# Loading the query weight of an expert layer by blocks of 32 partitions

## The chip, the cores and the metric

The kernel runs on one core of one Trainium2 chip. The metric is the device time of one execution in microseconds (us). A core has five engines that run their own instruction streams and meet at semaphores: TensorE (PE, with its weight loads shown as PEld), VectorE (DVE), ScalarE (ACT), GpSimd (POOL) and SyncE (SP), which here only issues transfers. Sixteen DMA engines move the data of all queues.

## The reference

Two layers of an encoder on 256 tokens of width 2048, in float32. Each layer adds the output of a mixer of three groups of attention heads, and then the output of an expert layer (PEER):

```
def peer_ffn(x, w_q, sub_keys, u, vv):
    q = (x @ w_q).reshape(bsz, s_len, 8, 2, 64)          # w_q: 2048 x 1024
    s = einsum('bshcd,cnd->bshcn', q, sub_keys)          # scores against 2 x 128 sub-keys
    ...                                                  # top 16 of 16384 experts for each head
    a = einsum('td,tkd->tk', xt, u[it])                  # u: 16384 x 2048
    return einsum('tk,tkd->td', gelu(a) * gt, vv[it])
```

The change touches only how `w_q` (8 MB for each layer) reaches the chip's memory.

## The kernel before

**Split products.** Every float32 operand of a product is split in two parts, `hi` (ACT, L251) and `lo` (DVE, L256; in part of the expert scan POOL). Three products (`hi` by `hi`, and each `hi` by the other's `lo`) make one float32 product.

**The job list.** The projections, the scan over the expert rows `u` and the start of the product with `v` are written as a list of jobs, which `run` works through. A job loads one tile `raw` of 128 partitions by 2048 elements (1 MB) and has two sub-steps, k = 0 and 1, each with half of the tile. Around the product of sub-step i the order in each engine's stream is: `hi` of sub-step i+2, `lo` of sub-step i+1, then the load of job j+2, then the matmuls of sub-step i. There are two `raw` buffers (in the scan every third tile comes from a third one), three `hi` and two `lo`. A load therefore waits until the last `lo` of two jobs before has read its buffer, and that `lo` waits for PE to be through with the `lo` two sub-steps before.

**The query projection.** In `proj_q` eight jobs load the query weight with `load_rows(..., strips=True)`, two k-tiles of 128 rows in each. The order of the rows is that of the transposed input: k-tile c holds the rows `a*512 + c*32 + j` for a = 0 to 3 and j = 0 to 31, so that the partition is `32*a + j`. In the first seven of the sixteen sub-steps PE also transposes a part of the normalised input (L335), which ACT and DVE split (L168, L169). Ahead of the stage stands the last step of the mixer's output projection: DVE adds the result to the residual (L837), ACT sums its squares (L277), and from these comes the scale that the first transposes need.

**The scan.** The next jobs load the expert rows `u`, 128 for each job, with four DMAs, one for each block of 32 partitions, each 32 partitions by four runs of 2 KB (L1333). DVE transposes blocks (L1268), and 24 matmuls for each sub-step follow (L1302, L1304). In the program's order the transpose of the first `u` tile stands on DVE ahead of the `lo` of the last query sub-step.

Of the kernel before, what the change touches and what calls it, by code (L numbers as in the profile page):

```python
# [33 lines left out]
P = 128  # L34
# [4 lines left out]
KT = D // P  # L39
# [55 lines left out]
def hybrid_parallel_heads_peer_encoder_kernel(ctx, tc, x, ln1, w_in, a_sink, b_rel_bias, c_q_norm, c_kv_norm,  # L95
# [4 lines left out]
    V, S, G, TE, SP = nc.vector, nc.scalar, nc.gpsimd, nc.tensor, nc.sync  # L100
# [162 lines left out]
    def load_rows(w, segs, c0, strips=False):  # L263

        def f(raw):
            wv = w.rearrange("(a c j) n -> c a j n", a=4, c=KT, j=32) if strips else \
                w.rearrange("(c p) n -> c p n", p=P)
            for k in range(2):
                o = k * 1024
                for s, n in segs:  # L270
                    SP.dma_start(raw[:, o:o + n], wv[c0 + k][..., s:s + n])
                    o += n
        return f
# [1277 lines left out]
```

## Time and profile before

| | |
|---|---|
| median of 3 runs | 3404.0 us (3401.57 to 3412.46) |
| the profiled execution's own time | 3402.82 us |
| its span, first to last instruction | 3401.0 us |
| mean granted clock of TensorE | 0.967 |
| PE / PEld busy | 91% / 84% |
| DVE / ACT / POOL busy | 72% / 50% / 54% |
| queue of SP's transfers | 434.08 MB, 52.3% of sixteen engines' span |

Busy shares are means over stages with different limits. The profile's page also gives the span in 40 slices; one slice is 85 us, about the length of one query projection, and there are two of these in the span, one for each layer.

### The profile page before, as it was taken

Reading aid. Unit: us, or ns where it says so; the run is one execution under the profiler, and the core shown is the slowest. Engines: PE = TensorE matmul, PEld = TensorE weight load, DVE = VectorE, ACT = ScalarE, POOL = GpSimd, SP = SyncE. Lnnn points to the kernel's source line nnn. Section 1 sums busy time; section 2 is a strip of 40 time slices with the busy share of each in tenths; the row PEclk is TensorE's granted clock in tenths of the full one; section 3 lists DMA queues with packets and bytes.
Section 4 is the critical chain, followed back from the end, with each engine's and each line's share of the span. In section 5 each row is a group of like instructions: output and inputs, shape, how many; then the busy total and the mean of one; then the engine's idle time right before and its main releaser. Section 6 shows DMA issues by size and latency. Waiting matters only on the chain. (4 is left out here: it accounts for less than half of the span.)

```text
span 3401.0 us, 58125 instructions
## 1 busy us (share of the span) xinstructions
PE 3100.9 (91%) x21677; PEld 2863.9 (84%) x21677; DVE 2442.1 (72%) x3613; ACT 1705.5 (50%) x2827; POOL 1825.2 (54%) x1135
## 2 busy tenths in 40 slices
PE   8998788989999987999999988799999999878998
PEld 8997688989899985888889977798899999867886
DVE  6576448997879865777766665489877788666776
ACT  5553433347657534555545544343475665345554
POOL 3010035678888883665530100256788888736663
PEclk9999889999999998999999999899999999889999
DMA  5677378889999996888745774688999999968885
GB/s 188 201 215 212 122 162 184 174 183 186 184 180 199 182 226 197 339 313 302 287 136 175 225 207 140 152 184 182 179 189 181 184 195 179 226 163 326 307 308 181
DMA packets 437750, 702.12 MB, mean 206 GB/s; under 512 B 103672, under 2 KB 236488, under 8 KB 413192
## 3 DMA queue, kind: packets, MB, share of 16 engines
q1 hardware_dynamic: 256016, 434.08, 52.3%
q0 software_dynamic: 112304, 228.13, 23.1%
q10 hardware_dynamic: 69064, 35.36, 4.3%
q8 instruction: 190, 3.11, 0.4%
q14 instruction: 176, 1.44, 0.2%
HBM read 627.95 MB, written 69.47 MB: 205 GB/s over the span
## 5 line engine op out<-in xcount | busy, mean ns | idle before, releaser
L1302 PE MATMUL acc<-x2h,hi 128*128 128x256 f32 x4096 | 1008.5, 285 | 28.2 <-ACT hi L251 15.3
L1044 POOL DMA_INDIRECT Gd<-g,idx x512 | 940.8, 1837 | 168.1 <-issue 151.6
L1302 PE MATMUL acc<-x2l,hi 128*128 128x256 f32 x4096 | 994.2, 281 | 0.0
L251 ACT ACTIVATE hi<-uT 128x1024 fp32r<-128x1024 f32 x512 | 543.6, 1062 | 729.0 <-DVE uT L1268 679.7
L1268 DVE STREAM_TRANSPOSE uT<-raw 128x1024 f32<-128x1024 f32 x512 | 635.2, 1241 | 324.9 <-DMA raw<-in_peer_u_dram 243.2
L1302 PEld LDWEIGHTS acc<-x2h,hi 128*128 128x128 f32 x4096 | 780.1, 190 | 34.7 <-ACT hi L251 20.0
L1302 PEld LDWEIGHTS acc<-x2l,hi 128*128 128x128 f32 x4096 | 779.8, 190 | 0.0
L1304 PE MATMUL acc<-x2h,lo 128*128 128x256 f32 x4096 | 581.4, 284 | 114.2 <-DVE lo L256 92.1
L1304 PEld LDWEIGHTS acc<-x2h,lo 128*128 128x128 f32 x4096 | 522.0, 190 | 134.5 <-DVE lo L256 104.6
L256 POOL TENSOR_TENSOR lo<-uT,hi 128x1024 fp32r<-128x1024 f32 x116 | 303.0, 2614 | 462.4 <-PE acc L1304 164.8
L166 DVE TENSOR_TENSOR vl<-vr,vh 128x1024 fp32r<-128x1024 f32 x356 | 426.2, 1224 | 145.9 <-ACT vh L165 140.4
L256 DVE TENSOR_TENSOR lo<-uT,hi 128x1024 fp32r<-128x1024 f32 x396 | 470.5, 1188 | 19.8 <-PE acc L1304 19.5
L165 ACT ACTIVATE vh<-vr 128x1024 fp32r<-128x1024 f32 x356 | 367.0, 1054 | 147.4 <-PE y L156 133.2
L256 DVE TENSOR_TENSOR lo<-raw,hi 128x1024 fp32r<-128x1024 f32 (+1 forms) x240 | 292.6, 1224 | 188.7 <-ACT hi L251 94.8
L152 PE MATMUL y<-vh,dh 128*128 128x512 f32 x1032 | 407.9, 395 | 20.3 <-ACT vh L165 14.1
L156 PE MATMUL y<-vh,dl 128*128 128x512 f32 x1032 | 406.5, 394 | 0.0
L251 ACT ACTIVATE hi<-raw 128x1024 fp32r<-128x1024 f32 (+1 forms) x240 | 246.6, 1035 | 317.7 <-DMA raw<-in_peer_w_q_dram 87.7
L1354 POOL DMA_INDIRECT vr<-in_peer_v_dram,iv x160 | 220.0, 1375 | 168.8 <-ACT vh L165 78.3
L161 PE MATMUL y<-vl,dh 128*128 128x512 f32 x1032 | 295.7, 393 | 0.2
L152 PEld LDWEIGHTS y<-vh,dh 128*128 128x128 f32 x1032 | 196.8, 191 | 65.0 <-ACT vh L165 23.9
L161 PEld LDWEIGHTS y<-vl,dh 128*128 128x128 f32 x1032 | 195.8, 190 | 43.4 <-DVE vl L166 2.4
L156 PEld LDWEIGHTS y<-vh,dl 128*128 128x128 f32 x1032 | 196.8, 191 | 41.1
(400 smaller groups left out, 4316.9 us busy)
## 6 DMA issues: line engine op xcount, KB each, us to landing
raw<-in_peer_u_dram SPq DMA_DIRECT2D x1024, 256.0 KB
raw<-in_w_in_dram SPq DMA_DIRECT2D x64, 512.0 KB
Gd<-z SPq DMA_DIRECT2D x32, 1024.0 KB
raw<-in_w_o_dram SPq DMA_DIRECT2D x32, 1024.0 KB
Gd<-at ACTq DMA_DIRECT2D x124, 256.0 KB
raw<-in_w_in_dram SPq DMA_DIRECT2D x64, 256.0 KB
raw<-in_peer_w_q_dram SPq DMA_DIRECT2D x32, 512.0 KB
raw<-in_w_in_dram SPq DMA_DIRECT2D x32, 416.0 KB
```

Of the source, the lines that this page charges most:

```text
L152: TE.matmul(o, lh, rh, start=start, stop=False, skip_group_check=shared)
L156: TE.matmul(o, ll, rh, start=False, stop=False, skip_group_check=shared)
L161: TE.matmul(o, lh, rl, start=False, stop=stop, skip_group_check=shared)
L165: S.activation(hi, src, AF.Copy)
L166: V.tensor_tensor(lo, src, R32(hi), op=OP.subtract)
L251: S.activation(view(h), src, AF.Copy)
L256: (eng or V).tensor_tensor(view(lo), src, R32(view(h)), op=OP.subtract)
L1044: d = G.indirect_dma_start(out=Gd[:], out_offset=bass.IndirectOffsetOnAxis(ap=r["idx"][:, hf, i:i + 1], axis=0), in_=r["g"][:, hf, i:i + 1 ...
L1268: V.transpose(t.rearrange("p (c e i) -> p c e i", c=8, e=4), rv.rearrange("p e (c j) -> p c e j", c=8))
L1302: TE.matmul(o, hi[:, c * P:(c + 1) * P], xx, start=k == 0 and c == 0 and n == 0, stop=False)
L1304: TE.matmul(o, lo[:, c * P:(c + 1) * P], xT(k * 8 + c)[0], start=False, stop=k == 1 and c == 7)
L1354: G.indirect_dma_start(out=raw, out_offset=None, in_=peer_v.rearrange("l e d -> (l e) d"), in_offset=at_(r[iv][:, c, m:m + 1]))
```

## The change

The query weight's job is loaded with four DMAs instead of two. Before, each k-tile is one DMA whose source has the dimensions 4 (a), 32 (j), 1024 (n) and whose destination is all 128 partitions of one half of `raw` (512 KB). After, each block a of 32 partitions is one DMA whose source has the dimensions 32 (j), 2 (k), 1024 (n) and whose destination is 32 partitions of both halves (256 KB). The same elements come to the same places. The other loads of `load_rows` stay as they are.

```diff
     def load_rows(w, segs, c0, strips=False):
 
         def f(raw):
-            wv = w.rearrange("(a c j) n -> c a j n", a=4, c=KT, j=32) if strips else \
-                w.rearrange("(c p) n -> c p n", p=P)
+            if strips:
+                (s, n), = segs
+                wa = w.rearrange("(a c j) n -> a j c n", a=4, c=KT, j=32)
+                for a in range(4):
+                    SP.dma_start(raw[32 * a:32 * a + 32, :].rearrange("p (k n) -> p k n", k=2),
+                                 wa[a][:, c0:c0 + 2, s:s + n])
+                return
+            wv = w.rearrange("(c p) n -> c p n", p=P)
             for k in range(2):
                 o = k * 1024
                 for s, n in segs:
```

## Rows read from the trace of the kernel before

**Rows 1.** The page's first part: busy us of each engine (share of the span).

```profile
PE 3100.9 (91%) x21677; PEld 2863.9 (84%) x21677; DVE 2442.1 (72%) x3613; ACT 1705.5 (50%) x2827; POOL 1825.2 (54%) x1135
```

**Rows 2.** Groups of ACT, 363 to 460 and 2077 to 2175: busy, mean | idle before, releasers.

```profile
L251 ACT ACTIVATE hi<-raw 128x1024 fp32r<-128x1024 f32 x16 | 16.9, 1058 | 57.6 <-DMA raw<-in_peer_w_q_dram 40.9 <-PE acc L142 5.5 <-PE acc L159 4.7
...
L251 ACT ACTIVATE hi<-raw 128x1024 fp32r<-128x1024 f32 x16 | 16.9, 1056 | 59.3 <-DMA raw<-in_peer_w_q_dram 46.9 <-PE acc L154 6.4 <-PE acc L142 6.1
```

**Rows 3.** Busy by stretch; last three columns: granted clock, DMA share, GB/s.

```profile
420.00:430.00 10.00, 8.50 (x48) 8.30 (x48) 2.45 (x2) 2.00 (x3) 0.00 (x0) 0.68 0.26 104
440.00:445.00 5.00, 3.48 (x28) 3.05 (x26) 1.23 (x1) 1.06 (x1) 0.00 (x0) 1.00 1.06 179
445.00:450.00 5.00, 0.00 (x0) 0.00 (x0) 0.00 (x0) 0.00 (x0) 0.00 (x0) 0.68 0.75 136
460.00:500.00 40.00, 40.00 (x342) 40.00 (x341) 22.36 (x21) 20.68 (x26) 20.57 (x9) 0.99 0.89 184
160.00:170.00 10.00, 10.00 (x70) 9.16 (x69) 5.38 (x9) 5.44 (x9) 0.00 (x0) 1.00 0.89 282
500.00:1200.00 700.00, 652.27 (x5566) 636.42 (x5565) 591.71 (x994) 380.89 (x761) 545.26 (x279) 1.00 0.94 183
```

**Rows 4.** ACT in order of time, layer 0: start, us, what [idle before <-releaser].

```profile
362.68 1.06 ACT L251 ACTIVATE hi<-raw 128x1024 fp32r<-128x1024 f32 x1 [5.46 <-PE acc L142]
367.73 1.06 ACT L251 ACTIVATE hi<-raw 128x1024 fp32r<-128x1024 f32 x1 [3.99 <-DVE xt L837]
...
370.53 0.58 ACT L277 ACTIVATE acc<-xt 128x512 f32<-128x512 f32 x1
...
387.02 1.06 ACT L251 ACTIVATE hi<-raw 128x1024 fp32r<-128x1024 f32 x1 [4.31 <-DMA raw<-in_peer_w_q_dram]
...
412.30 1.06 ACT L251 ACTIVATE hi<-raw 128x1024 fp32r<-128x1024 f32 x1 [2.63 <-DMA raw<-in_peer_w_q_dram]
419.40 1.06 ACT L251 ACTIVATE hi<-raw 128x1024 fp32r<-128x1024 f32 x1 [6.03 <-DMA raw<-in_peer_w_q_dram]
...
450.09 1.06 ACT L251 ACTIVATE hi<-raw 128x1024 fp32r<-128x1024 f32 x1 [8.73 <-DMA raw<-in_peer_w_q_dram]
```

**Rows 5.** SP's issues in order of time, layer 0.

```profile
354.21 1.33 SPq L271 DMA_DIRECT2D raw<-in_peer_w_q_dram  x2
...
378.27 1.14 SPq L271 DMA_DIRECT2D raw<-in_peer_w_q_dram  x2
...
436.90 2.25 SPq L1333 DMA_DIRECT2D raw<-in_peer_u_dram  x5
```

**Rows 6.** DVE in order of time, layer 0.

```profile
364.91 2.72 DVE L837 SCALAR_TENSOR_TENSOR xt<-acc,rg,xt 128x512 f32<-128x512 f32 x4
...
453.23 1.25 DVE L1268 STREAM_TRANSPOSE uT<-raw 128x1024 f32<-128x1024 f32 x1 [10.62 <-DMA raw<-in_peer_u_dram]
454.40 1.18 DVE L256 TENSOR_TENSOR lo<-raw,hi 128x1024 fp32r<-128x1024 f32 x1
```

**Rows 7.** PE in order of time, layer 0.

```profile
373.47 1.97 PE L335 MATMUL mi<-CP,xs 128*128 128x128 f32 x8 [10.20 <-ACT xs L327]
...
386.63 0.37 PE L152 MATMUL acc<-x2h,hi 128*128 128x256 f32 x1
...
389.88 0.37 PE L152 MATMUL acc<-x2h,hi 128*128 128x256 f32 x1
...
455.64 0.58 PE L142 MATMUL acc<-x2h,lo 128*128 128x256 f32 x1 [3.65 <-DVE lo L256]
...
460.48 0.28 PE L1302 MATMUL acc<-x2h,hi 128*128 128x256 f32 x1
...
463.28 0.28 PE L1302 MATMUL acc<-x2h,hi 128*128 128x256 f32 x1
```

**Rows 8.** PE in order of time, layer 1.

```profile
2087.34 1.97 PE L335 MATMUL mi<-CP,xs 128*128 128x128 f32 x8 [10.87 <-ACT xs L327]
...
2174.61 0.28 PE L1302 MATMUL acc<-x2h,hi 128*128 128x256 f32 x1
```

## The prediction

> **What bounds the kernel now.** I read the page first. PE is busy for 3100.9 us, 91% [rows 1], so on average this is a PE-bound kernel; but the change sits in two stages of about 100 us, and what it is worth is read there. The groups of ACT in these stages come next: the 16 `hi` splits of the query weight work for 16.9 us and stand behind idle time of 57.6 us in layer 0 and 59.3 us in layer 1, of which the weight's DMA ended 40.9 and 46.9 us [rows 2]. So ACT waits for weights, and PE for ACT. The view by stretch says why. While only the query weight is in flight, the mean busy share of the sixteen DMA engines is 0.26 at 104 GB/s [rows 3]: 4 of 16 engines' worth, 26 GB/s for each. Compare 160 to 170 us, where the mixer's weights come in over 128 partitions: 0.89 and 282 GB/s. ACT in order of time shows the same as a beat: `hi` starts at 362.68 and 367.73, 5.05 us apart [rows 4], and 512 KB in 5.05 us is 104 GB/s. (The releasers named there, PE and DVE, only happened to end at those moments; the beat is the transfer's.) PE's own work for a k-tile is shorter: 389.88 − 386.63 = 3.25 us with its four transposes, and 463.28 − 460.48 = 2.80 us for the same 24 matmuls without them [rows 7]. The stage is bound by its transfers.
>
> **Part 1: the rate.** Removed in each layer are 16 DMAs of 512 KB whose source has 4 as its outer dimension; added are 32 of 256 KB with 32 outside, to 32 partitions each. The trace has just this form in the expert rows (32 partitions, four DMAs for a 1 MB tile), with runs of 2 KB where the new ones have 4 KB. These load at 184 GB/s with a share of 0.89, so 184 / 0.89 = 207 GB/s if the engines were full [rows 3]. The other end is 16 engines × 26 = 416 GB/s. I take 207, as the nearest row in form: 1 MB in 5.0 us instead of 10.1.
>
> [...]
>
> What lies around the transfer: a load issued at 378.27 to an empty queue is split at 387.02 [rows 5, 4], 8.75 us, of which 5.05 is transfer and 3.7 fixed. A new 1 MB tile then is ready 3.7 + 5.0 = 8.7 us after its first issue, at the same moment as the first half-tile now, but whole. SP issues four DMAs in 4 × 2.25 / 5 = 1.8 us [rows 5] instead of two in 1.14; behind them stand only the next loads, which wait for a buffer anyway: nothing.
>
> **Part 2: the start of the stage.** The first load goes out at 354.21 [rows 5]; its tile is ready at 362.9, both `hi` are through by 365.0 (1.06 each), the first `lo` (1.18, [rows 6]) by 365.2, and the four residual additions (2.72 us, [rows 6]) end at 367.9. The squares follow them; the last, 0.58 us, is done at 368.5. Now it is done at 370.53 + 0.58 = 371.1 [rows 4], since ACT's squares stand behind the second `hi`, which waits for its DMA until 367.73. PE restarts 2.6 us earlier, at 370.9 instead of 373.47 [rows 7]. At 416 GB/s the tile would be ready at 360.4, the additions would start at PE's last matmul (373.47 − 10.20 = 363.27), and the squares would end at 366.6: 4.5 us.
>
> **Part 3: the sixteen k-tiles.** Now, from PE's restart to the first expert matmul: 460.48 − 373.47 = 87.0 us in layer 0, 2174.61 − 2087.34 = 87.3 in layer 1 [rows 7, 8]. Without waits: the restart and k-tiles 0 to 3, which already run at PE's pace, 389.88 − 373.47 = 16.4; two more with transposes, 2 × 3.25 = 6.5; ten without, 28.0; together 50.9 us. That takes tiles of 2.80 us, from a stretch with a granted clock of 0.99 [rows 3]; the 0.68 of 420 to 430 us comes after waits of PE, and these go.
>
> What is late next, in each layer:
> - The buffer loop. Two tiles are in flight; a load goes out 1.4 us into the first k-tile of the tile two before (after its `lo`), is ready 8.7 later and split 1.1 later: 11.3 us against 4 × 2.80 = 11.2 of PE. It is in balance; three turns of it: 0.5 us.
> - The tables that ACT loads in the middle of the stage (528 KB): they set the beat back now, 419.40 − 412.30 = 7.10 instead of 5.05 [rows 4], so 2.0 us. The loop has no slack to hide it.
> - The end. The `lo` of the last k-tile stands on DVE behind the transpose of the first expert tile [rows 6], and PE waits for it (3.65 us now, [rows 7]). That tile is issued 1.4 us into k-tile 12, is ready at 10.1, transposed at 11.35 and the `lo` done at 12.8 (1.25 and 1.18 with hand-overs); PE wants it at 3 × 2.80 + 0.25 = 8.65: 4.2 us.
>
> Sum: 50.9 + 6.7 = 57.6 us. The gain is 87.0 + 2.6 − 57.6 = 32.0 in layer 0 and 32.3 in layer 1, 64.3 us in all. The profiled execution's own time is 3402.8, 1.2 us under the median of 3404.0; so 3338.5 on the one, 3339.7 on the other.
>
> **Part 4: does it stay?** After the stage comes the scan: its first tiles meet the last `lo` as they do now (one tile ready, two on their way), PE is at 40.00 of 40 us from the first expert matmul on, and its loads run at a share of 0.89 [rows 3], so there is a little room. Routing starts with the end of the projection and moves along. I book no loss.
>
> **Rivals.**
> *More: 416 GB/s.* For it: 4 KB runs, and 26 GB/s for each engine as now. Against it: the 207 of the same form. It gives 4.5 us at the start, no loop loss, tables at half (1.0), the end unchanged: 87.0 + 4.5 − 50.9 − 5.2 = 35.4, two layers 71: 3332.
> *Slower landing.* With other traffic beside them the two forms got 136 to 179 GB/s at 440 to 450 us [rows 3], and the last half-tile took until 450.09 [rows 4]. At 136, a tile takes 7.7 us. The third tile goes out at 378.27 − 2.6 = 375.7 and is ready at 387.1, the eighth 5 × 7.7 + 2 later at 427.7, the first expert tile at 432.7; 2.7 us to the last `lo`, 2.6 of matmuls: 438.0, a gain of 22.5 for each layer: 3358.
> *Given back in the scan.* If its loads bind it (0.94 share from 500 to 1200 us, PE busy 652 of 700, [rows 3]), only their earlier start counts: k-tile 12 would begin at 370.9 + 16.4 + 6.5 + 6 × 2.8 + 2.5 = 413.1, the first issue at 414.5 against 436.90 [rows 5], 22.4 for each layer: 3358. Against it: PE without a gap at the scan's start.
> *No wider than before.* If the new DMAs also run on four engines, each tile must land whole, 13.8 us after its issue: the last square slips from 371.1 to 373.7, the beat stays: up to 2.6 for each layer, 3408. The expert loads' share of 0.89 speaks against it.
> *Slower than before: the fixed 3.7 us paid four times.* Were the DMAs of one tile to run one after the other, a tile would take 4 × (3.7 + 1.25) = 19.8 us; six of them from 378.3 on end at 497, and the first expert matmul comes at about 507: 47 us for each layer, 3497. It decides once the added cost of each DMA exceeds (10.1 − 5.0) / 4 = 1.3 us. Against it: the expert rows come in four such DMAs and keep up at 184 GB/s.
> [...]
>
> **How the numbers follow.** Forecast 0.55; 416 GB/s 0.18; slower landing 0.12; given back 0.08; no wider 0.03; four times the fixed cost 0.04. The time is 3339. The first has its own range of 3330 to 3347, for losses from 3 to 11 us instead of 6.7 for each layer. From 3322 (PE without any wait in these stages) to 3364 (beyond the two rivals at 3358) all but about 0.1 is held. A measurement of this kernel can tell some 0.3% (10 us) from no change: faster 0.93, within 0.03 (no wider), slower 0.04.
>
> **What would show it.** In the stage: a DMA share well above 0.26; both `hi` of a tile back to back, with one wait for each tile instead of two; k-tiles of PE 2.8 to 3.3 us apart; the first expert matmul some 32 us earlier in layer 0 and 64 in layer 1. It is wrong if the share stays near 0.26, if the `hi` still come 5 us apart, or if the shift at the scan's start is there and gone at its end.

## The result, and the profile after

The changed kernel takes 3327.7 us (median of 4 runs, 3324.4 to 3331.6) against 3402.8 for the kernel before (4 runs, 3400.7 to 3412.5): a ratio of 0.977, 95% interval 0.974 to 0.979. That is 11 us less than the forecast of 3339. It lies inside the whole range of 3322 to 3364, but below the forecast's own range of 3330 to 3347 and nearer to the 3332 of the rival of 416 GB/s. Run again with four other kernels beside it, it took 3337.0 against 3406.4, ratio 0.978 (0.976 to 0.980). The gain is 69 to 75 us, where 64 had been forecast.

The profiled execution took 3324.4 us, with a span of 3322.6. The lines below answer to those of before; L270 is the new load of the query weight, L1274, L1308 and L1310 are the old L1268, L1302 and L1304.

Busy time by stretch, changed kernel (PE, PEld, DVE, ACT, POOL; then granted clock, DMA share, GB/s):

```profile
354.00:360.00 6.00, 6.00 (x28) 4.82 (x27) 2.45 (x2) 2.17 (x5) 0.00 (x0) 1.00 0.95 216
375.00:395.00 20.00, 20.00 (x175) 20.00 (x174) 11.98 (x18) 10.94 (x18) 0.00 (x0) 1.00 0.70 156
395.00:410.00 15.00, 13.20 (x114) 12.99 (x113) 6.25 (x8) 4.78 (x7) 0.00 (x0) 1.00 1.03 229
425.00:465.00 40.00, 39.22 (x331) 38.75 (x331) 23.30 (x22) 20.89 (x27) 19.59 (x9) 1.00 0.91 185
465.00:1165.00 700.00, 656.01 (x5594) 641.26 (x5593) 594.41 (x995) 382.32 (x763) 545.07 (x276) 0.99 0.95 185
...
2101.60:2106.50 4.90, 4.90 (x23) 4.90 (x24) 3.98 (x6) 2.10 (x5) 0.00 (x0) 0.50 1.05 210
```

Where the query weight alone loads, the engines are now busy for 0.95 of the time at 216 GB/s, where it was 0.26 at 104 [rows 3]. The share grew 3.7 times and the rate only twice, because each packet now takes longer. The weight moves in packets of 4 KB (the part of one row that one k-tile needs), and over layer 0's stage the median packet took 0.16 us before and takes 0.31 now, worked out from the packets' records: four packets are under way at once for nine tenths of 420 to 430 us before (five for the rest), and four engines with 4 KB in 0.16 us are 102 GB/s, sixteen with 4 KB in 0.31 us are 211. PE works without a gap from 375 to 395 us.

The groups of ACT, layer 0 and layer 1 (busy, mean | idle before, releasers):

```profile
L251 ACT ACTIVATE hi<-raw 128x1024 fp32r<-128x1024 f32 x16 | 16.5, 1054 | 20.9 <-DMA raw<-in_peer_w_q_dram 18.5 <-DVE lo L256 1.5 <-ACT x2h L168 0.6
...
L251 ACT ACTIVATE hi<-raw 128x1024 fp32r<-128x1024 f32 x16 | 16.5, 1054 | 20.4 <-DMA raw<-in_peer_w_q_dram 17.6 <-PE acc L159 1.9 <-ACT x2h L168 0.6
```

The idle time of ACT ahead of its 16 splits went from 57.6 and 59.3 us [rows 2] to 20.9 and 20.4. Of what is left, one wait still reaches PE: ACT's 6.67 us ahead of 408.77, as 1.80 us at 409.88 in the lines of PE below.

ACT in order of time, layer 0:

```profile
359.94 2.01 ACT L251 ACTIVATE hi<-raw 128x1024 fp32r<-128x1024 f32 x2 [3.82 <-DMA raw<-in_peer_w_q_dram]
...
364.94 0.60 ACT L283 ACTIVATE acc<-xt 128x512 f32<-128x512 f32 x1
...
379.64 1.06 ACT L251 ACTIVATE hi<-raw 128x1024 fp32r<-128x1024 f32 x1 [2.27 <-DMA raw<-in_peer_w_q_dram]
...
408.77 2.01 ACT L251 ACTIVATE hi<-raw 128x1024 fp32r<-128x1024 f32 x2 [6.67 <-DMA raw<-in_peer_w_q_dram]
```

SP's issues in order of time, layer 0:

```profile
353.13 5.12 SPq L270 DMA_DIRECT2D raw<-in_peer_w_q_dram  x5
...
372.65 7.77 SPq L270 DMA_DIRECT2D raw<-in_peer_w_q_dram  x7
...
412.25 3.66 SPq L1339 DMA_DIRECT2D raw<-in_peer_u_dram  x8
```

A tile issued at 353.13 is split from 359.94 on, 6.8 us later, one issued at 372.65 at 379.64, 7.0 later; both halves can be split back to back. The beat of 5.05 us for each half [rows 4] is gone.

PE in order of time, layer 0, then layer 1:

```profile
367.89 1.97 PE L341 MATMUL mi<-CP,xs 128*128 128x128 f32 x8 [5.70 <-ACT xs L333]
...
409.88 0.38 PE L152 MATMUL acc<-x2h,hi 128*128 128x256 f32 x1 [1.80 <-ACT hi L251]
...
422.23 0.39 PE L142 MATMUL acc<-x2h,lo 128*128 128x256 f32 x1 [1.78 <-DVE lo L256]
...
424.94 0.28 PE L1308 MATMUL acc<-x2h,hi 128*128 128x256 f32 x1
...
2049.62 1.97 PE L341 MATMUL mi<-CP,xs 128*128 128x128 f32 x8 [5.82 <-ACT xs L333]
...
2101.60 0.58 PE L142 MATMUL acc<-x2h,lo 128*128 128x256 f32 x1 [3.34 <-DVE lo L256]
...
2106.46 0.41 PE L1308 MATMUL acc<-x2h,hi 128*128 128x256 f32 x1
```

DVE in order of time, layer 0, the end of the stage:

```profile
419.83 1.25 DVE L1274 STREAM_TRANSPOSE uT<-raw 128x1024 f32<-128x1024 f32 x1 [4.09 <-DMA raw<-in_peer_u_dram]
421.00 1.18 DVE L256 TENSOR_TENSOR lo<-raw,hi 128x1024 fp32r<-128x1024 f32 x1
```

From PE's restart to the first expert matmul it is 424.94 − 367.89 = 57.0 us and 2106.46 − 2049.62 = 56.8, where it was 87.0 and 87.3 [rows 7, 8]; the gap ahead of the restart is 5.70 and 5.82 instead of 10.20 and 10.87. Up to the first expert matmul this gives 87.0 − 57.0 + 10.20 − 5.70 = 34.5 in layer 0 and 35.5 in layer 1: 70 of the 78.4 us between the two profiled executions. The scan of layer 0 takes 3.3 us longer than before and that of layer 1 9.1 less, which gives most of the other 8; a scan's length spreads by as much between executions of one kernel (the table below).

### The profile page after: what moved, and what is told of

Same layout as the page of the kernel before. It is cut to its first block, busy times and chain, and to the rows that moved or that the text cites. A ratio compares the mean times of both kernels' runs of the same rounds, so it can differ in the third digit from the quotient of the medians.

```text
span 3322.6 us, 58212 instructions
## 1 busy us (share of the span) xinstructions
PE 3085.5 (93%) x21677; PEld 2852.7 (86%) x21677; DVE 2439.9 (73%) x3613; ACT 1701.7 (51%) x2827; POOL 1805.3 (54%) x1135
## 3 DMA queue, kind: packets, MB, share of 16 engines
q1 hardware_dynamic: 256912, 434.08, 54.3%
## 5 line engine op out<-in xcount | busy, mean ns | idle before, releaser
L1308 PE MATMUL acc<-x2h,hi 128*128 128x256 f32 x4096 | 1012.2, 286 | 31.0 <-ACT hi L251 15.3
L1050 POOL DMA_INDIRECT Gd<-g,idx x512 | 928.8, 1814 | 171.1 <-issue 151.7
L1308 PE MATMUL acc<-x2l,hi 128*128 128x256 f32 x4096 | 997.2, 282 | 0.3 <-issue 0.3
L1274 DVE STREAM_TRANSPOSE uT<-raw 128x1024 f32<-128x1024 f32 x512 | 634.9, 1240 | 303.1 <-DMA raw<-in_peer_u_dram 217.3
L1308 PEld LDWEIGHTS acc<-x2h,hi 128*128 128x128 f32 x4096 | 783.5, 191 | 37.2 <-ACT hi L251 20.0
L1308 PEld LDWEIGHTS acc<-x2l,hi 128*128 128x128 f32 x4096 | 781.9, 191 | 1.3 <-issue 1.3
L1310 PE MATMUL acc<-x2h,lo 128*128 128x256 f32 x4096 | 583.5, 285 | 99.2 <-DVE lo L256 76.3
L1310 PEld LDWEIGHTS acc<-x2h,lo 128*128 128x128 f32 x4096 | 523.2, 191 | 119.1 <-DVE lo L256 87.1
L256 DVE TENSOR_TENSOR lo<-uT,hi 128x1024 fp32r<-128x1024 f32 x396 | 470.0, 1187 | 21.4 <-PE acc L1310 11.3
```

The costliest lines, as they stand in the source:

```text
L256: (eng or V).tensor_tensor(view(lo), src, R32(view(h)), op=OP.subtract)
L1050: d = G.indirect_dma_start(out=Gd[:], out_offset=bass.IndirectOffsetOnAxis(ap=r["idx"][:, hf, i:i + 1], axis=0), in_=r["g"][:, hf, i:i + 1 ...
L1274: V.transpose(t.rearrange("p (c e i) -> p c e i", c=8, e=4), rv.rearrange("p e (c j) -> p c e j", c=8))
L1308: TE.matmul(o, hi[:, c * P:(c + 1) * P], xx, start=k == 0 and c == 0 and n == 0, stop=False)
L1310: TE.matmul(o, lo[:, c * P:(c + 1) * P], xT(k * 8 + c)[0], start=False, stop=k == 1 and c == 7)
```

## The experiments

The theory: a DMA whose source has 4 as its outer dimension runs on four of the sixteen engines (0.26 × 16 = 4.2 [rows 3]), and that alone made the stage slow. The rivals: it is the number or size of the DMAs, or that one DMA spans both k-tiles; and how far the rate goes is set by engines and rows, or by how many partitions a transfer reaches. A second group of runs asks what is left of the stage.

**Eight DMAs, each of one k-tile.** They have the outer dimension of the change and the k-tiles of before.

```diff
-                for a in range(4):
-                    SP.dma_start(raw[32 * a:32 * a + 32, :].rearrange("p (k n) -> p k n", k=2),
-                                 wa[a][:, c0:c0 + 2, s:s + n])
+                for k in range(2):
+                    for a in range(4):
+                        SP.dma_start(raw[32 * a:32 * a + 32, k * 1024:(k + 1) * 1024], wa[a][:, c0 + k, s:s + n])
```

> Eight DMAs for each query tile: 32 partitions by one k-tile, 128 KB, k = 0 first; the first `hi` of a tile waits for four of them alone. Outer dimension 32, as in the change, but each DMA is within one k-tile, as before it. If the outer dimension is what counts (32: all sixteen engines; 4: four): DMA share over 0.9 while only this weight loads, first `hi` of the stage at or a little before that of the changed kernel (360 us), time 3320 to 3335. If it counts that one DMA spans both k-tiles, or if each DMA pays its fixed cost by itself: 8 x 1.3 us and more for each tile, 3380 to 3450.

Measured: 3328.2 us, ratio 0.977 (0.972 to 0.981), as the change. (One of its four executions took 3307.6 us; why is not known.) Busy by stretch, the middle one that of the first tile's packets:

```profile
356.00:362.00 6.00, 6.00 (x27) 4.83 (x26) 2.89 (x3) 4.51 (x6) 0.00 (x0) 1.00 0.63 176
357.40:362.60 5.20, 5.20 (x24) 4.17 (x23) 2.45 (x2) 3.12 (x4) 0.00 (x0) 1.00 0.76 215
...
396.00:411.00 15.00, 15.00 (x131) 15.00 (x131) 6.44 (x6) 5.30 (x5) 0.00 (x0) 1.00 0.86 215
```

Spanning both k-tiles does not matter, and eight DMAs cost no more than four: the rival of a fixed cost paid for each DMA falls. The share of over 0.9 that was expected is not there in these stretches, yet the first tile's 1 MB takes 5.1 us from its first packet to the end of its last, as in the change (5.0). Its first half is split 4.1 us after the first issue (356.47 to 360.54), since it waits for four of the DMAs alone.

**Four DMAs with an outer dimension of 2.** As many and as large as in the change.

```diff
...
+                wc = w.rearrange("(a c j) n -> c a j n", a=4, c=KT, j=32)
+                for k in range(2):
+                    for b in range(2):
+                        SP.dma_start(raw[64 * b:64 * b + 64, k * 1024:(k + 1) * 1024],
+                                     wc[c0 + k][2 * b:2 * b + 2, :, s:s + n])
...
```

> Four DMAs of 256 KB for each query tile, as many and as large as in the change, but each of one k-tile and two blocks of 32 partitions: the source's outer dimension is 2. If the outer dimension sets the number of engines: 2 of 16, share 0.13, 52 GB/s, 1 MB in 20 us instead of 10.1 before, for each layer some 7 tiles x 10 us more than before, time 3520 to 3560. If the number and size of DMAs is what helps: like the changed kernel, 3325 to 3340.

Measured: 3553.9 us, ratio 1.045 (1.042 to 1.048). Busy by stretch, and ACT in order of time:

```profile
358.00:368.00 10.00, 5.67 (x25) 4.23 (x23) 1.23 (x1) 0.00 (x0) 0.00 (x0) 0.92 0.13 52
```

```profile
368.02 1.06 ACT L251 ACTIVATE hi<-raw 128x1024 fp32r<-128x1024 f32 x1 [10.41 <-DMA raw<-in_peer_w_q_dram]
378.12 1.06 ACT L251 ACTIVATE hi<-raw 128x1024 fp32r<-128x1024 f32 x1 [9.04 <-DMA raw<-in_peer_w_q_dram]
```

Share 0.13, 52 GB/s, 10.1 us for 512 KB: two engines' worth (0.13 × 16 = 2.1). A packet takes 0.16 us, as before the change. With the rows of before (4: 0.26) and of the change (32: 0.95) this shows that in these loads the outer dimension sets how many engines' worth of transfer there is, 2.1, 4.2 and 15.2; what it leaves open is the rate of sixteen engines, for which the next run and the loads to 128 partitions further down were made.

**Eight DMAs of 16 partitions.** The outer dimension is 16, and the rows are again of 4 KB.

```diff
...
+                wa = w.rearrange("(a c b j) n -> a b j c n", a=4, c=KT, b=2, j=16)
+                for a in range(4):
+                    for b in range(2):
+                        p0 = 32 * a + 16 * b
+                        SP.dma_start(raw[p0:p0 + 16, :].rearrange("p (k n) -> p k n", k=2),
+                                     wa[a][b][:, c0:c0 + 2, s:s + n])
...
```

> Eight DMAs for each query tile: 16 partitions by both k-tiles, 128 KB, outer dimension 16, so again sixteen engines, with rows of 4 KB as in the change. If the rate is set by how many partitions one transfer reaches (32: 210 to 227 GB/s; so 16: half, 104 to 114): share near 1 at 104 to 114 GB/s, 1 MB in 9 to 10 us, time 3385 to 3415, near the kernel before. If engines or row length set it: 210 GB/s or more, 3320 to 3340. With some overlap of neighbouring transfers: in between.

Measured: 3361.0 us, ratio 0.989 (0.986 to 0.992), in between. Busy by stretch, and ACT:

```profile
356.00:365.00 9.00, 8.05 (x35) 6.16 (x33) 2.45 (x2) 1.99 (x3) 0.00 (x0) 1.00 1.05 160
...
380.00:400.00 20.00, 18.71 (x157) 18.12 (x156) 9.81 (x15) 9.12 (x16) 0.00 (x0) 1.00 0.90 123
```

```profile
365.47 2.00 ACT L251 ACTIVATE hi<-raw 128x1024 fp32r<-128x1024 f32 x2 [7.48 <-DMA raw<-in_peer_w_q_dram]
```

The engines are full (1.05) and yet move 160 / 1.05 = 152 GB/s, later 123 / 0.90 = 137. The first tile takes 6.9 us, against 5.0 with 32 partitions, and a packet 0.43 us at the median, against 0.31. So 16 partitions are slower than 32 here, with the engines full and the same rows, but not by half. The eight DMAs are not the cause, for the first experiment had eight of 128 KB as well.

**The four blocks in another order.**

```diff
-                for a in range(4):
+                for a in (0, 2, 1, 3):
```

> The change with its four blocks issued in the order 0, 2, 1, 3 instead of 0, 1, 2, 3, the same bytes. If a transfer is held to the part of memory that its partitions reach and the queue runs strictly in order: the same rate (210 to 227 GB/s) and time, within 5 us of the changed kernel's 3328. [...]

Measured: 3323.9 us, ratio 0.978 (0.975 to 0.980). Busy by stretch, and ACT:

```profile
354.00:360.00 6.00, 6.00 (x27) 4.86 (x26) 2.45 (x2) 2.49 (x4) 0.00 (x0) 1.00 0.86 193
```

```profile
360.24 2.01 ACT L251 ACTIVATE hi<-raw 128x1024 fp32r<-128x1024 f32 x2 [3.74 <-DMA raw<-in_peer_w_q_dram]
```

193 / 0.86 = 224 GB/s, and the first tile, issued at 353.50, is split 6.7 us later instead of 6.8: the order makes no difference that these show. Time and rate are those that were expected; what holds the rate there is not shown by this run.

**What is left of the stage: the base, and two edits.**

> The changed kernel again, beside the next three, as their base: 3320 to 3332 (3327.7 before), and a measure of how far one and the same kernel spreads.

Measured: 3337.0 us, ratio 0.978 (0.976 to 0.980), above what was expected. Its five executions reach from 3331.4 to 3337.3, the four of the first measurement from 3324.4 to 3331.6. The first edit puts the `lo` of the last query k-tile ahead of the first expert transpose:

```diff
-            prep_a(i + 2)
-            prep_b(i + 1)
+            if i + 2 < len(flat) and flat[i + 2][0] in heads and flat[i + 1][0] not in heads:
+                prep_b(i + 1)
+                prep_a(i + 2)
+            else:
+                prep_a(i + 2)
+                prep_b(i + 1)
...
+        heads.append(len(jobs))
         for q in range(NQ):
```

> The change, and at the one place where the scan begins the `lo` of the last query k-tile stands on DVE ahead of the transpose of the first expert tile, not behind it. My account of the end of the stage (PE waits for this `lo`, 1.78 us in layer 0 and 3.34 in layer 1, and the tile after the wait runs at the lower clock): the last k-tile follows the one before without a wait, the first expert matmul comes 2.1 us earlier in layer 0 and 4 to 5 in layer 1, in all 4 to 7 us less than the changed kernel beside it, less than the spread of runs but visible in the trace. If the first expert tile's own landing is the limit: the wait moves to the first expert matmul and under 2 us is gained.

Measured: 3334.3 us, ratio 0.978 (0.976 to 0.980), 2.7 us under the base where 4 to 7 had been expected; its executions reach from 3328.6 to 3347.9. The second edit moves the tables:

```diff
-            S.dma_start(r["cl"], c_lst)
...
             s_sb = [rp.tile([P, 8, 2, P], F32, name="s_sb", tag=f"s{hf}") for hf in range(2)]
+            S.dma_start(r["cl"], c_lst)
```

> The change, and the 528 KB of tables that ACT loads in the middle of the stage are loaded after the projection, when routing has begun. My account (the tables push back a query tile in layer 0, PE waits 1.80 us at 409.88 and then runs k-tile 12 at the lower clock, 4.5 us instead of 2.8): no wait of PE in the stage of layer 0 but that of the last `lo`, first expert matmul 3 to 4 us earlier there; the time 0 to 4 us less than the changed kernel, for the tables then lie beside the scan's first tiles. If the buffer loop itself is short: the wait stays.

Measured: 3333.6 us, ratio 0.978 (0.976 to 0.980), 3.4 us under the base.

> Both edits, the last `lo` first and the tables late. If the two waits are all that is left of the stage: restart to first expert matmul 51 to 53 us in both layers instead of 57, the sum 4 to 10 us less than the changed kernel, 3317 to 3324. If the waits turn into one another: no less than the better one alone.

Measured: 3337.0 us, ratio 0.978 (0.976 to 0.980): all four are alike, and the 4 to 10 us that were expected of both edits are not there. Yet in the stage the edits do what they should. PE's waits (us in total, times, longest), base, layer 0:

```profile
PE mi L341 <- ACT xs L333: 6.1, 1, 6.1
PE acc L142 <- DVE lo L256: 4.2, 1, 4.2
PE acc L159 <- DVE lo L256: 0.4, 1, 0.4
PE acc L152 <- ACT hi L251: 0.3, 1, 0.3
```

And with both edits, layer 0:

```profile
PE mi L346 <- ACT xs L338: 5.9, 1, 5.9
PE acc L1313 <- ACT hi L256: 1.8, 1, 1.8
```

The wait for the last `lo` is gone, and a wait for the first expert tile has come in its place, 1.8 us here and 0.5 in layer 1. PE begins the scan 4 to 5 us earlier in each layer, counted from its restart; the scan's end does not follow. Worked out from the first and last starts of each group, in us, layer 0 / layer 1:

| | restart to first expert matmul | that to the last one | first transpose of the scan to its last matmul |
|---|---|---|---|
| before | 87.0 / 87.3 | 846.2 / 847.9 | 853.5 / 854.6 |
| changed | 57.0 / 56.8 | 849.5 / 838.8 | 854.6 / 846.1 |
| changed, again | 58.1 / 57.1 | 848.5 / 846.2 | 855.7 / 852.8 |
| last `lo` first | 53.8 / 52.3 | 850.4 / 861.4 | 852.9 / 863.8 |
| tables late | 57.1 / 54.3 | 846.6 / 850.1 | 853.2 / 855.2 |
| both | 53.4 / 52.3 | 852.8 / 857.6 | 855.2 / 860.0 |

What PE wins at the scan's start by not waiting for the last `lo` is not seen at its end. The two kernels with the last `lo` first take 855.5 us on the mean from the first expert matmul to the last, the other four 846.7; counted from the first transpose, 858.0 and 853.2. The difference shrinks but does not vanish, and the spread is as large: the profiled execution of the kernel with the last `lo` first is the slowest of its five (3347.9), and the scans of the other kernels with these experts, further up and down, take from 841.6 to 853.5 us. That the scan is paced from its first tile on is possible and not shown. What gives the time back stays open. The wait for `hi` that is put down to the tables was 1.80 us in the changed kernel's layer 0, 0.3 in the base beside these runs, 0.8 with the last `lo` first and 1.6 in the next kernel; with the tables late it is gone in both runs.

**The first expert tile sooner.**

```diff
-                alloc=(lambda: r["up"].tile([P, D], F32, name="raw", tag="raw")) if q % 3 == 1 and q < NQ - 1 else None)
+                alloc=(lambda: r["up"].tile([P, D], F32, name="raw", tag="raw")) if q % 3 == 0 and q < NQ - 1 else None)
```

> The change, and the third buffer of the scan serves tiles 0, 3, 6, ... instead of 1, 4, 7, ...: the first expert tile no longer waits for the `lo` of k-tile 13 and is issued right behind the last query tile. In all kernels run so far the scan ends 846 to 864 us (mostly 853 to 855) after the first expert tile is transposed, however early PE began. If the scan is paced from its first tile on: that transpose 3 to 6 us earlier in each layer, no wait for the last `lo`, the scan's end as much earlier, time 6 to 12 us less than the changed kernel (3328 to 3337), so 3318 to 3329. If the gain is given back in the scan: the transpose earlier, the end not, time as the changed kernel.

Measured: 3331.6 us, ratio 0.978 (0.976 to 0.980), no gain. SP, busy by stretch, and ACT, layer 0:

```profile
407.87 0.79 SPq L1339 DMA_DIRECT2D raw<-in_peer_u_dram  x2
```

```profile
405.00:420.00 15.00, 13.41 (x115) 13.21 (x115) 4.53 (x4) 4.02 (x4) 0.00 (x0) 1.00 1.05 214
```

```profile
421.76 1.06 ACT L251 ACTIVATE hi<-uT 128x1024 fp32r<-128x1024 f32 x1 [4.31 <-DVE uT L1274]
```

The tile is issued 38.2 us after PE's restart (407.87 − 369.70) instead of 44.4 (412.25 − 367.89), but transposed at 420.4, 50.7 us after it instead of 51.9. In between the engines are full, and the last two query tiles and this one come one after the other (410.71, 415.44, 420.40): once it is issued early, the queue sets its landing. PE still waits 2.0 us for the last `lo` in layer 0 and 3.1 in layer 1. The question that this run was meant for, whether the scan's end follows its first tile, stays open, because that tile did not move.

**Loads to 128 partitions, and their control.** The three kernels here read the weight's rows in another order than the input has. They do not compute the reference, and serve for times alone.

```diff
...
+                wv = w.rearrange("(c p) n -> c p n", p=P)
+                for k in range(2):
+                    SP.dma_start(raw[:, k * 1024:(k + 1) * 1024], wv[c0 + k][:, s:s + n])
...
```

> Two DMAs of 512 KB for each query tile, as before the change, each of one k-tile to all 128 partitions, with an outer dimension of 128: rows c*128 to c*128 + 127 of the weight, which is another order of rows than the input has, so the queries and the chosen experts are others; the amount of work is nearly the same. If the partitions that a transfer reaches set its rate: 300 GB/s or more with full engines (32 partitions: 227; 16: 137 to 152), first tile split 5.0 to 5.5 us after its issue instead of 6.8, the stage's waits gone but for the last `lo`; the time within 10 us of the changed kernel, since PE sets the pace there already. If sixteen engines give 227 at any width above 32: 6.8 us.

Measured: 3363.0 us, ratio 0.988 (0.985 to 0.990). Busy by stretch, the first one taken where the engines are full, and ACT:

```profile
355.25:356.90 1.65, 1.65 (x9) 1.33 (x8) 1.41 (x2) 0.87 (x2) 0.00 (x0) 1.00 1.02 412
356.00:360.00 4.00, 4.00 (x19) 3.23 (x18) 2.19 (x3) 2.12 (x2) 0.00 (x0) 1.00 0.61 200
...
380.00:400.00 20.00, 20.00 (x175) 20.00 (x174) 11.58 (x16) 10.47 (x15) 0.00 (x0) 1.00 0.54 190
```

```profile
356.63 1.06 ACT L251 ACTIVATE hi<-raw 128x1024 fp32r<-128x1024 f32 x1 [0.78 <-DMA raw<-in_peer_w_q_dram]
358.20 1.06 ACT L251 ACTIVATE hi<-raw 128x1024 fp32r<-128x1024 f32 x1 [0.51 <-PE acc L156]
```

Where the engines are full, in the first stretch, they move 412 GB/s; the two longer stretches (0.61 and 0.54) have pauses of the queue in them. A packet takes 0.16 us at the median, as on four engines, and the first tile 3.6 us, against 5.0 with 32 partitions and 6.9 with 16. These two DMAs also have the number, size and destination of those before the change. Beside the outer dimension of the source (128 instead of 4) only the rows differ, and the share went from 0.26 to 1.02: of all pairs here this one isolates the outer dimension best. The first half-tile is split 3.8 us after its issue at 352.85, and the second by 358.20 at the latest. The stage takes 52.9 and 53.9 us. The time is 35 us above the changed kernel's 3327.7, where within 10 had been expected; the control has the change's own loads with the same rows:

```diff
-                wa = w.rearrange("(a c j) n -> a j c n", a=4, c=KT, j=32)
+                wa = w.rearrange("(c a j) n -> a j c n", a=4, c=KT, j=32)
```

> A control for the kernel with loads to 128 partitions, whose time was 3363 although its stage took 53 us and not 57: the change's four DMAs to 32 partitions, but with the same other rows of the weight (c*128 to c*128 + 127), so with the same other queries and experts. If the other experts cost the 30 us (the stretch from the scan's end to the next query load took 774 us against 755 to 760): this one also 3355 to 3370. If the wide loads themselves cost it: 3320 to 3340.

Measured: 3371.9 us, ratio 0.9905 (0.9875 to 0.9934). So the other rows, and with them the other experts, cost those 35 us and more, not the loads. The trace shows where: from layer 0's scan to the next query load it is 775 us here and 774 with the wide loads, against 755 to 761 in the kernels of the table. A packet takes 0.32 us here, as in the change, so the other rows are not what makes the wide loads quick.

> The loads to 128 partitions with the other rows again, beside its control. If loads to 128 partitions in place of 32 save what their stage shows (3 to 5 us for each layer, first expert tile transposed 2 to 3 us earlier): 2 to 8 us under the control. If the stage is past being bound by the rate: within 3 us of it.

Measured: 3365.7 us, ratio 0.989 (0.986 to 0.992), 6 us under its control; the intervals overlap, so a gain from wide loads is likely and not shown. In the stages it can be seen: 54.8 and 53.9 us against 59.7 and 56.5, and 1.8 us less ahead of each restart (4.1 against 5.9 and 6.0). With the order of rows that this kernel needs, one k-tile as one transfer has blocks of rows that lie apart, and so an outer dimension of 4, as before the change; no way round this was tried.

## Why the prediction was right, point by point

- **The bound.** Four engines' worth of transfer set the stage. This is shown: the outer dimensions 2, 4, 32 and 128 give a share of 0.13, 0.26, 0.95 and 1.02, and with 2 and 4 each engine moves about 26 GB/s (52 / 2 and 104 / 4).
- **The rate.** I took 207 GB/s from the expert rows, and 5.0 us for a tile, against 416. The first tile's packets take 5.0 us, which is 209 GB/s. The row nearest in form was the right one, and what counts in the form is, in these runs, the number of partitions: 416 is near what sixteen engines gave with 128 partitions (412), not with 32. The mixer's weights over 128 partitions, at 282 / 0.89 = 317 [rows 3], stay below these 412.
- **A tile's way round the transfer.** This was the term mis-sized: 8.7 us from issue to split, measured 6.8 to 7.0. I had carried the 3.7 us around a transfer on four engines over to sixteen; with the 5.0 and 5.4 us that the packets of these two tiles take it is 1.8 and 1.6. On two engines it is 13.4 − 10.1 = 3.3 (first issue at 354.6, split at 368.02). The packets of the first load before the change show what the term had in it: the first packet starts 1.4 us after the issue instead of 1.0, the first half-tile takes 6.2 us and not the 5.05 of the beat, and from its last packet to the split it is 0.9 us instead of 0.8. Why a first transfer on few engines is slower than its beat stays open.
- **The start.** Because of that the first tile is there (359.94, split by 361.95) before PE's last matmul of the projection ends (362.19), so the restart gains 4.5 us, not 2.6, and 5.05 in layer 1. It is the value that I had given the rival of 416 GB/s: the tile is there in time, but through the shorter way round the transfer and not through the rate. These 4.4 us are most of the difference between the forecast gain to the first expert matmul, 64.3, and the measured 70.
- **The sixteen k-tiles.** Forecast 57.6 us from restart to first expert matmul, measured 57.0 and 56.8. The buffer loop costs nothing (11.3 was 9.4 with the shorter way, under PE's 11.2). The tables cost 1.8 us of waiting and then 1.5 in a slow k-tile in layer 0, 0.3 in the run repeated and nothing in layer 1, for 2.0 in each layer forecast. The last `lo` costs 1.8 and 3.3 us of waiting, 4.2 and 3.6 in the run repeated, for 4.2 forecast. That an earlier issue of the first expert tile would end this wait, as my account of it implies, was wrong: issued 6 us sooner it came 1 us sooner, for the queue is full there. And the clock was put at nothing, since PE's waits were to go: in layer 1 the matmuls after the last wait took 2.2 us longer than in layer 0, at a granted clock of 0.50. So the sum of 6.7 us over the pace of PE came out (6.1 and 5.9) with parts that were not those forecast, which is in part luck.
- **Does it stay?** Yes, for the 70 us: the scan after it is as long as before within its spread. The profiled executions have the first expert matmul 35.5 us earlier in layer 0 and 68.2 in layer 1, and the end 78.4. But the rival "given back in the scan" fits what comes after: the edits that took another 4 to 5 us out of each stage won nothing clear of the spread in the whole, and where it went is not shown.
- **The other rivals.** No wider than before: refuted by the share of 0.95. A fixed cost for each DMA: refuted by eight DMAs for each tile at the same time. Slower landing: the first tiles landed faster than forecast, and the gain up to the first expert matmul is 34.5 and 35.5 us, not 22.5.

By partitions, 16 gave 151 GB/s over the first tile (1 MB in 6.9 us), 32 gave 209, and 128 gave 412 with full engines. So 16 partitions give more than the half of 32 that one of the expectations had. Transfers behind one another may overlap there, which is not shown; blocks 0 and 2 in a row won nothing over 0 and 1 (first tile split after 6.7 us and 6.8).

## What to carry to other kernels

Look at the DMA share of a stage beside its GB/s: here a share of 0.26, with one queue loading and an engine waiting for it, was four engines' worth of transfer at 26 GB/s each and not a slow memory, which gave 216 GB/s to the changed load, and the outer dimension of the transfer set it. Do not read a full share as the full rate: with sixteen engines at work, 16, 32 and 128 partitions gave about 150, 210 and 410 GB/s. Price a new form of transfer by the row nearest to it in partitions, not by engines times the rate of one, and take the fixed part from a row with as many engines. And once PE sets the pace of a stage, follow a further saving to the end of the next stage before booking it: 9 to 10 us won at the start of two scans were not found at their ends.

## What was not expected

After a short wait of PE the matmuls behind it can lose nearly as much again: after 1.80 us of idling k-tile 12 took 4.3 us instead of 2.80 (409.88 to 414.21; granted clock 0.71 and 0.60 in the two halves of 410 to 415 us). After 3.34 us in layer 1 the matmuls up to the scan took 4.9 us (2101.6 to 2106.5) at a granted clock of 0.50; the same matmuls took 2.7 us in layer 0. The 1.78 us of layer 0 at 422 had no such effect: the steps after it come 0.35 us apart, at a granted clock of 1.00. Nor is the length of the wait enough to tell: in the kernel with the first expert tile sooner a wait of 1.6 us had no such effect (granted clock 1.00 from 410 to 420 us), and one of 2.0 us was followed by a granted clock of 0.62.
